# Weights packed in order of use, x and vectors turned by the host, and longer runs of high and low products

## The chip, the cores and the metric

The kernel runs on one core of a Trainium2 chip. The metric is the device time of one execution in microseconds. Five engines work side by side: PE (TensorE) multiplies matrices, PEld is its loading of the stationary operand, DVE (VectorE) and ACT (ScalarE) do elementwise work, POOL (GpSimd) and SP mostly start transfers (DMA). Each engine takes its instructions in order, and waits for others through semaphores.

## The reference, cut to what matters

```python
# T = 256 positions, D = 2048, D_FF = 5504, everything float32, one layer
h = rms_norm(x, norm_mix);  proj = h @ w_in                      # 2048 x 9216
uv, qkv, gates = split(proj)
u, v = split(gelu(uv));  y_a = u * (w_s @ layer_norm(v) + b_s)   # 8 groups, chunks of 128
y_b = neighbourhood_attn(q, k, v, rpb)                           # 16 heads on a 4 x 64 grid
merged = sigmoid(g_a) * (y_a @ w_branch[:1024]) + sigmoid(g_b) * (y_b @ w_branch[1024:])
x = x + merged @ w_out
up = conv3(rms_norm(x, norm_ffn) @ w_up) + conv_b                # 2048 x 11008
x = x + (silu(gate) * val) @ w_down                              # 5504 x 2048
out = rms_norm(x, norm_final)
```

Some 61 million weights are used once each.

## The kernel before

**Products in three parts.** TensorE multiplies in a rounded format (float32r). To keep float32's precision, weights and activations are each split into a high part, which is the value rounded, and a low part, which is the rest: `w = whi + wlo`, `x = xh + xl`. A product is then `xh whi + xl whi + xh wlo`. For weights ACT writes `whi` (L127) and DVE writes `wlo` (L128); for x the same is done at L318 and L325, with the norm's weight `gmix` multiplied in.

**Pieces.** All weights are cut into pieces of two k, that is of 2 x 128 rows by up to 512 columns, numbered in the order in which they are used. `begin(i)` opens piece i: it issues loads up to five pieces ahead of the splits (`load_to`, SP's queue, `wraw` with 5 buffers), splits up to three pieces ahead (`split_to`, `whi` and `wlo` with 4 buffers each), and runs what was noted for this piece with `at(i, f)`: transposes, evictions, softmax and so on. For the first five pieces the noted work comes ahead of the splits. In `load_to`, `preload[i]` is further loads that go into SP's queue ahead of piece i's weights.

**Two kinds of groups.** A group is one block of output columns over all k. In a *natural* group ("nat", `products`, L198 to L200) the activations are stationary and the weights stream 512 columns: per k and half of the positions three products, each of 512 columns. In a *weight-stationary* group ("ws", `spread_products`, L177 and L181) the weights are stationary: for each of up to four blocks of 128 columns a *high* product streams `xh` and `xl` together (512 columns, L177) and a *low* product streams `xh` alone (256 columns, L181). Per k all blocks' high products come first, then all blocks' low ones; for the last k of a group it is low, then high. Each block has its own PSUM bank. Weight-stationary are two u groups, four qk groups and 22 groups of the up-projection, with 16 k each; the last of these has two blocks instead of four.

**The start.** x is loaded in eight chunks of 256 columns with positions on partitions (`load_x`, L243, tile `xs`). Each chunk is turned by four transposes on TensorE (`x_chunk`, L338) into a PSUM bank, and split from there. Ahead of it TensorE runs transposes of the identity (`keep_awake`, L283), nine and then eight. The norm's weights, the convolution's and its bias are loaded as rows and turned likewise (`vec_T`, L257), and so is W_s (`turn_ws`, L870). The sum of squares of x for the norm is taken by ACT from `xs` at pieces 5 to 8 (`x_stats`).

Of the kernel before, what the change touches and what calls it, by code (L numbers as in the profile page):

```python
# [15 lines left out]
T = 256  # L16
# [22 lines left out]

LOAD_AHEAD = 5  # L40
# [3 lines left out]

@with_exitstack
def trunk_kernel(ctx, tc, x, norm_mix, w_in, ln_g, ln_b, w_s, b_s, rpb, w_branch, w_out,
                 norm_ffn, w_up, conv_k, conv_b, w_down, norm_final, out):
# [27 lines left out]
    pieces = []  # L75

    def plan(src, row0, nk, blocks):
        first = len(pieces)
        for k in range(0, nk, 2):
            pieces.append((src, row0 + k * 128, min(2, nk - k), blocks))  # L80
        return first
# [6 lines left out]
    def load_to(n):  # L88
        while n_loaded[0] < min(n, len(pieces)):
            i = n_loaded[0]  # L90
            n_loaded[0] += 1
            if i in preload:
                for f in preload[i]:
                    f()
            src, r0, kn, (c0, cn, nb, cs) = pieces[i]
            w = wpool.tile([128, 2, 512], F32, name="wraw", bufs=LOAD_AHEAD)
            ld = src.shape[-1]
            if i == 0:
                for k in range(kn):
                    if k:  # L100
                        load_x(256, 256)
                    nc.sync.dma_start(w[:, k, :cn], src[r0 + k * 128:r0 + (k + 1) * 128, c0:c0 + cn])
            elif nb == 1:
                nc.sync.dma_start(
                    w[:, :kn, :cn],
                    bass.AP(tensor=src.tensor, offset=src.offset + r0 * ld + c0,
                            ap=[[ld, 128], [128 * ld, kn], [1, cn]]))
            else:
                for b in range(nb):
                    nc.sync.dma_start(  # L110
                        w[:, :kn, b * cn:(b + 1) * cn],
                        bass.AP(tensor=src.tensor, offset=src.offset + r0 * ld + c0 + b * cs,
                                ap=[[ld, 128], [128 * ld, kn], [1, cn]]))
            raw[i] = w

    def split_to(n):
        while n_split[0] < min(n, len(pieces)):
            i = n_split[0]
            n_split[0] += 1
            src, r0, kn, (c0, cn, nb, cs) = pieces[i]  # L120
# [3 lines left out]
            m = cn * nb  # L124

            def part(k):
                nc.scalar.activation(h[:, k, :m], w[:, k, :m], AF.Copy)  # L127
                nc.vector.tensor_sub(l[:, k, :m], w[:, k, :m], h[:, k, :m].bitcast(F32))  # L128
# [15 lines left out]
    midway = {}  # L144
# [5 lines left out]
    def begin(i):  # L150
        cur[0] = i
        load_to(i + LOAD_AHEAD)
        if i == 0:
            gm_turn()
            split_to(1)
# [7 lines left out]
    def natural(src, row0, nk, c0, cn, acts, done):  # L163
        n0 = plan(src, row0, nk, (c0, cn, 1, 0))
        return ("nat", n0, nk, cn, acts, done)

    def stationary(src, row0, nk, c0, cn, nb, cs, acts, done):
        n0 = plan(src, row0, nk, (c0, cn, nb, cs))
        return ("ws", n0, nk, cn * nb, acts, done)

    def spread_products(g, ps, i, h, l):
# [30 lines left out]
    def run_group(g, by_block=0):  # L202
# [4 lines left out]
        for i in range(n0, n1 - by_block):  # L207
# [7 lines left out]
            for b in range(nblk):  # L215
                if b == 1 and i in midway:
                    midway.pop(i)()
# [22 lines left out]
    xs = xin.tile([128, NT, D], F32)  # L240

    def load_x(c0, n):
        nc.sync.dma_start(xs[:, :, c0:c0 + n],  # L243
                          bass.AP(tensor=x.tensor, offset=x.offset + c0, ap=[[D, 128], [128 * D, NT], [1, n]]))

    def rows(src, off, n):
        return bass.AP(tensor=src.tensor, offset=src.offset + off, ap=[[128, n], [1, 128]])

    def vec_T(name, src, off, n, dst, queue=None):
        t = xin.tile([n, 128], F32, name=name)  # L250

        def load():
            (queue or nc.sync).dma_start(t, rows(src, off, n))

        def go():
            p = bank()
            nc.tensor.transpose(p[:, :n], t, ident[:n, :n])  # L257
            nc.vector.tensor_copy(dst, p[:, :n])
        return load, go

    gmix = const.tile([128, KD], F32)
    gffn = const.tile([128, KD], F32)
    ck = const.tile([128, 4, 2 * NF], F32)
    gm_load, gm_turn = vec_T("gm_rows", norm_mix, 0, KD, gmix, nc.scalar)
    gm_load()
    ws_raw = xin.tile([128, GMG, 128], F32)

    def load_ws():
        nc.sync.dma_start(ws_raw, bass.AP(tensor=w_s.tensor, offset=w_s.offset,
                                          ap=[[128, 128], [128 * 128, GMG], [1, 128]]))  # L270
# [15 lines left out]
    late = [vec_T("gf_rows", norm_ffn, 0, KD, gffn)]  # L286
    for j in range(3):
        late.append(vec_T(f"ck_rows{j}", conv_k, j * 2 * DFF, 2 * NF, ck[:, j, :]))
    late.append(vec_T("cb_rows", conv_b, 0, 2 * NF, ck[:, 3, :]))
# [26 lines left out]
    def split_pair(p, dsts, gs):  # L316
# [3 lines left out]
        for kk in range(2):  # L320
# [12 lines left out]
    def x_chunk(c):  # L333
        p = bank()
        for kk in range(2):
            k = c * 2 + kk
            for t in range(NT):
                nc.tensor.transpose(p[:, kk * T + t * 128:kk * T + (t + 1) * 128],  # L338
                                    xs[:, t, k * 128:(k + 1) * 128], ident)
        split_pair(p, xT[2 * c:2 * c + 2], gmix[:, 2 * c:2 * c + 2])  # L340
# [9 lines left out]
    def ev_vg(j):  # L350
        def done(ps, i):
            if j == 0:
                at(i + 2, lambda: gelu_v(ps, i))
# [444 lines left out]
    w_in2 = w_in[0]  # L798
    w_br, w_o, w_u, w_d = w_branch[0], w_out[0], w_up[0], w_down[0]
    xt = lambda k: xT[k]  # L800
    g_vg = [natural(w_in2, 0, KD, V0 + j * 512, 512, xt, ev_vg(j)) for j in range(2)]
    g_u = [stationary(w_in2, 0, KD, U0 + j * 512, 512, 1, 0, xt, ev_u(j)) for j in range(2)]
    def g_va(j):
        return natural(w_in2, 0, KD, VA0 + j * 512, 512, xt, ev_va(j))

    def g_qk(j):
        return stationary(w_in2, 0, KD, Q0 + j * 256, 256, 2, K0 - Q0, xt, ev_qk(j))

    def g_gate(br, j):
        return natural(w_in2, 0, KD, (GA0, GB0)[br] + j * 512, 512, xt, ev_gate(br, j))  # L810

    def g_branch(br, j):
        return natural(w_br, br * 1024, 8, j * 512, 512, lambda k: yT[br * 8 + k], ev_branch(br, j))
# [6 lines left out]
    g_o = [natural(w_o, 0, KD, j * 512, 512, lambda k: mg["mT"][k], ev_out(j)) for j in range(4)]  # L820
    g_up = []
    for f in range(0, NF, 2):
        nb = min(2, NF - f)
        g_up.append(stationary(w_u, 0, KD, f * 128, nb * 128, 2, DFF, lambda k: rs["h", k], ev_up(f, nb)))
    g_dn = [natural(w_d, 0, NF, j * 512, 512, lambda k: ff["a"][k], ev_down(j) if j < 3 else finish) for j in range(4)]
# [24 lines left out]
    for c in range(4):  # L850
        at(5 + c, lambda c=c: x_stats(c))
    at(9, x_norm)
    at(12, lambda: st1.__setitem__("rb", bcast_cols("rb1", st1["r"])))
# [7 lines left out]
    preload[9] = [load_ws]  # L861
    for n, (dst, src) in enumerate(((gm_pool["g"], ln_g), (gm_pool["b"], ln_b),
                                    (gm_pool["bs"].rearrange("p a b -> p (a b)"), b_s))):
        preload[10 + n] = [lambda dst=dst, src=src: nc.sync.dma_start(
            dst, bass.AP(tensor=src.tensor, offset=src.offset, ap=[[0, 128], [1, GMW]]))]

    def turn_ws(h):
        p = bank()
        for g in range(4):
            nc.tensor.transpose(p[:, g * 128:(g + 1) * 128], ws_raw[:, h * 4 + g, :], ident)  # L870
        nc.vector.tensor_copy(gm_pool["wsT"][:, h * 4:h * 4 + 4, :].rearrange("p a b -> p (a b)"), p)

    at(14, lambda: turn_ws(0))
    at(15, lambda: turn_ws(1))
    preload[13] = [ld for ld, _ in late]
    for n, (_, f) in enumerate(late):
        at(17 + n // 2, f)
# [71 lines left out]
    for g in g_dn[:3]:  # L949
# [5 lines left out]
_INS = ['x', 'norm_mix', 'w_in', 'gm_ln_g', 'gm_ln_b', 'gm_w_s', 'gm_b_s', 'na_rpb', 'w_branch', 'w_out',  # L955
        'norm_ffn', 'w_up', 'conv_k', 'conv_b', 'w_down', 'norm_final']
# [24 lines left out]
```

## Time and profile before

| | |
|---|---|
| median of 3 runs | 1339.79 us (1339.69 to 1340.09) |
| span of the profiled execution, first to last instruction | 1338.0 us |
| its own time beside the span | not listed apart; the median lies 1.8 us above the span |
| PE busy | 1327.1 us, 99% |
| DVE, ACT, POOL busy | 871.8, 719.0, 104.8 us |
| moved by DMA | 259.36 MB, mean 194 GB/s |
| mean granted TensorE clock | 0.998 |
| first product of a piece starts | 6.49 us |
| first weight-stationary product starts | 56.96 us |

In rows of the timeline the first number is the start in us from the span's start, the second the time from the start of the first instruction of the row to the end of the last; `x4` means four instructions in the row. Matmuls overlap, since the next one starts while the last one drains. Names are tiles: `bank<-h,whi` writes a PSUM bank from the split activations and the weights' high part. In square brackets stand the idle time ahead and what ended it.

### The profile page before, as it was taken

The page shows a single profiled execution, that of the slowest core. Times are in us where ns is not written, and L with a number is a line of the kernel's source. Part 1 is how long each engine was busy: PE and PEld are TensorE (multiplying, and loading weights), DVE is VectorE, ACT ScalarE, POOL GpSimd, SP SyncE. Part 2 cuts the span into 40 slices and gives each one's busy share as a digit, 9 for nine tenths or more (in the row PEclk, how much of TensorE's full clock was granted, in tenths as well). Part 3 has the DMA queues.
Part 4 walks back from the last instruction along what each step waited for, and adds up shares of the span by engine and source line. Part 5 has one row for each costly group of instructions (what it writes and reads, how often), then busy time and mean ns, then how long its engine had stood idle before and what let it go on. Part 6 is the DMA issues. An engine that isn't in the chain of part 4 may idle for free.

```text
span 1338.0 us, 18985 instructions
## 1 busy us (share of the span) xinstructions
PE 1327.1 (99%) x6863; PEld 1127.8 (84%) x6863; DVE 871.8 (65%) x1256; ACT 719.0 (54%) x1059; POOL 104.8 (8%) x192
## 2 busy tenths in 40 slices
PE   9999999999999999999999999999999999999997
PEld 7888888888888888888888888888888888888885
DVE  6476567767564645555778777777777775545454
ACT  6665557577444444555655555555555554434342
POOL 0241055530000000000000000000000000000000
PEclk9999999999999999999999999999999999999999
DMA  9766775655666666665565656565656557656662
GB/s 329 223 188 179 215 224 173 205 173 161 196 182 194 190 192 222 204 197 183 185 192 182 196 177 200 177 196 182 192 186 190 172 181 225 209 186 208 188 198 101
DMA packets 194030, 259.36 MB, mean 194 GB/s; under 512 B 12952, under 2 KB 124432, under 8 KB 193936
## 3 DMA queue, kind: packets, MB, share of 16 engines
q1 hardware_dynamic: 189648, 250.31, 59.8%
q0 software_dynamic: 3968, 7.30, 2.3%
q8 instruction: 54, 0.88, 0.3%
q10 hardware_dynamic: 320, 0.53, 0.1%
q14 instruction: 40, 0.33, 0.1%
HBM read 253.90 MB, written 2.10 MB: 191 GB/s over the span
## 4 chain that ended last, share of the span: by engine, by line
PE 99%; DMA 0%; DVE 0%; ACT 0%; SPq 0%; issue 0%; DVEq 0%
PE bank L177 31%; PE bank L198 17%; PE bank L200 17%; PE bank L199 17%; PE bank L181 16%; PE bank L563 1%; DMA wraw<-in_w_in_dram 0%; PE bank L613 0%; PE bank L439 0%; PE bank L659 0%; PE bank L603 0%; PE bank L701 0%; PE bank L338 0%; DVE x L791 0%; PE bank L310 0%; PE bank L870 0%
## 5 line engine op out<-in xcount | busy, mean ns | idle before, releaser
L128 DVE TENSOR_TENSOR wlo<-wraw,whi 128x1024 fp32r<-128x1024 f32 (+1 forms) x473 | 570.6, 1211 | 395.2 <-ACT whi L127 381.4
L127 ACT ACTIVATE whi<-wraw 128x1024 fp32r<-128x1024 f32 (+1 forms) x473 | 491.8, 1044 | 414.9 <-PE bank L199 280.4
L177 PE MATMUL bank<-h,whi 128*128 128x512 f32 x1760 | 479.2, 395 | 0.0
L177 PEld LDWEIGHTS bank<-h,whi 128*128 128x128 f32 x1760 | 301.9, 189 | 41.5
L181 PEld LDWEIGHTS bank<-h,wlo 128*128 128x128 f32 x1760 | 267.2, 189 | 35.6
L181 PE MATMUL bank<-h,wlo 128*128 128x256 f32 x1760 | 276.6, 281 | 0.0
L198 PE MATMUL bank<-whi,h 128*128 128x512 f32 x384 | 152.4, 397 | 0.1
L199 PE MATMUL bank<-whi,h 128*128 128x512 f32 x384 | 149.9, 390 | 0.4 <-DVE h L325 0.3
L200 PE MATMUL bank<-wlo,h 128*128 128x512 f32 x384 | 149.9, 390 | 0.0
L199 PE MATMUL bank<-whi,a 128*128 128x512 f32 x344 | 133.8, 389 | 0.0
L200 PE MATMUL bank<-wlo,a 128*128 128x512 f32 x344 | 133.8, 389 | 0.0
L198 PE MATMUL bank<-whi,a 128*128 128x512 f32 x344 | 133.8, 389 | 0.0
L199 PEld LDWEIGHTS bank<-whi,h 128*128 128x128 f32 x384 | 72.3, 188 | 15.5 <-DVE h L325 1.2
L200 PEld LDWEIGHTS bank<-wlo,h 128*128 128x128 f32 x384 | 72.2, 188 | 15.6 <-DVE wlo L128 0.4
L198 PEld LDWEIGHTS bank<-whi,h 128*128 128x128 f32 x384 | 72.2, 188 | 15.0 <-ACT whi L127 0.5
L727 ACT ACTIVATE tc<-ta,ck 128x256 f32<-128x256 f32 x86 | 47.1, 595 | 69.8 <-DVE ta L725 69.8
L199 PEld LDWEIGHTS bank<-whi,a 128*128 128x128 f32 x344 | 64.6, 188 | 13.5
L200 PEld LDWEIGHTS bank<-wlo,a 128*128 128x128 f32 x344 | 64.6, 188 | 13.4
L198 PEld LDWEIGHTS bank<-whi,a 128*128 128x128 f32 x344 | 64.6, 188 | 13.3
L943 POOL DMA_DIRECT2D gfin<-in_norm_final_dram x4 | 2.2, 548 | 646.5 <-DVE tc L738 539.2
L730 DVE SCALAR_TENSOR_TENSOR tc<-ta,ck,tc 128x255 f32<-128x255 f32 x86 | 41.4, 481 | 14.4 <-ACT tc L727 14.4
L198 PE MATMUL bank<-whi,m 128*128 128x512 f32 x128 | 50.1, 392 | 0.0
(157 smaller groups left out, 1092.7 us busy)
## 6 DMA issues: line engine op xcount, KB each, us to landing
wraw<-in_w_up_dram SPq DMA_DIRECT2D x336, 256.0 KB, 3.2
wraw<-in_w_in_dram SPq DMA_DIRECT2D x111, 512.0 KB, 3.7
wraw<-in_w_down_dram SPq DMA_DIRECT2D x84, 512.0 KB, 4.6
wraw<-in_w_in_dram SPq DMA_DIRECT2D x66, 256.0 KB, 3.5
wraw<-in_w_branch_dram SPq DMA_DIRECT2D x32, 512.0 KB, 4.5
wraw<-in_w_out_dram SPq DMA_DIRECT2D x32, 512.0 KB, 3.9
xs<-in_x_dram SPq DMA_DIRECT2D x8, 256.0 KB, 7.2
vw<-va POOLq DMA_DIRECT2D x32, 64.0 KB, 5.2
```

The source lines that it names most:

```text
L127: nc.scalar.activation(h[:, k, :m], w[:, k, :m], AF.Copy)
L128: nc.vector.tensor_sub(l[:, k, :m], w[:, k, :m], h[:, k, :m].bitcast(F32))
L177: nc.tensor.matmul(p, h[:, k - k0, b * 128:(b + 1) * 128], acts(k), start=k == 0, stop=k == nk - 1)
L181: nc.tensor.matmul(p[:, :T], l[:, k - k0, b * 128:(b + 1) * 128], acts(k)[:, 0, :], start=False, stop=False)
L198: nc.tensor.matmul(p, xh, h[:, kk, :m], start=st, stop=False)
L199: nc.tensor.matmul(p, xl, h[:, kk, :m], start=False, stop=False)
L200: nc.tensor.matmul(p, xh, l[:, kk, :m], start=False, stop=sp)
L563: nc.tensor.matmul(o, Q[s][:, c], k.rearrange("p (r c) -> p r c", r=ROWS)[:, :, k0:k0 + UNION], start=n == 0, stop=n == 1)
L727: nc.scalar.activation(v, u, AF.Identity, scale=ck[:, 1, ch:ch + 1], bias=ck[:, 3, ch:ch + 1])
L730: nc.vector.scalar_tensor_tensor(v[:, 1:], u[:, :T - 1], ck[:, 0, ch:ch + 1], v[:, 1:], op0=OP.mult, op1=OP.add)
L943: nc.gpsimd.dma_start(fin["g", j], bass.AP(tensor=norm_final.tensor, offset=norm_final.offset + j * 512, ap=[[0, 128], [1, 512]]))
```

## The change

The host (numpy) now lays the inputs out before the launch:

- All weights lie in one flat array in the order of the pieces, and within a piece each partition's two k lie together, so one partition's part is one run of 4 KB (in before rows of 2 KB, or of 1 KB in groups with two column blocks). A piece is one transfer, where groups with two column blocks took two.
- x comes turned (`x_turned`, k on partitions, loaded by k). `x_chunk` splits straight from SBUF; the transposes of x are gone. The statistics still need x by rows, which is loaded a second time, in two transfers of 1 MB ahead of the weights of pieces 10 and 11. They are taken at pieces 9 to 12 instead of 5 to 8, the norm at 13 instead of 9, and the first gelu moves from two pieces behind its group to six.
- The vectors come turned in one array: 16 columns at the start on ACT's queue, the rest ahead of the weights of piece 16. W_s comes turned, ahead of piece 12. `vec_T` and `turn_ws` are gone with their transposes and copies.
- In a weight-stationary piece the high products of both k come together, then the low ones; in every second piece low ones first, then high ones.

```diff
-        for k in range(k0, min(k0 + 2, nk)):
-            for f in (high, low) if k < nk - 1 else (low, high):
+        for f in (high, low) if (i - n0) % 2 == 0 else (low, high):
+            for k in range(k0, min(k0 + 2, nk)):
                 f(k)
...
+            cn = size // kn
+            parts = range(kn) if i == 0 else [slice(0, kn)]
+            for k in parts:
+                k0, k1 = (k, k + 1) if i == 0 else (0, kn)
+                if i == 0 and k:
+                    load_x(1)
+                src = bass.AP(tensor=weights.tensor, offset=weights.offset + off + k0 * cn,
+                              ap=[[size, 128], [cn, k1 - k0], [1, cn]])
+                nc.sync.dma_start(w[:, k0:k1, :cn], src)
...
+    def load_x(k0, n=1):
+        nc.sync.dma_start(xk[:, k0:k0 + n, :], x_turned[:, k0:k0 + n, :])
...
-    def x_chunk(c):
-        p = bank()
-        for kk in range(2):
-            k = c * 2 + kk
-            for t in range(NT):
-                nc.tensor.transpose(p[:, kk * T + t * 128:kk * T + (t + 1) * 128],
-                                    xs[:, t, k * 128:(k + 1) * 128], ident)
-        split_pair(p, xT[2 * c:2 * c + 2], gmix[:, 2 * c:2 * c + 2])
+    def x_chunk(c, part=(0, 1)):
+        split_pair(xk[:, 2 * c:2 * c + 2, :].rearrange("p k t -> p (k t)"), xT[2 * c:2 * c + 2],
+                   gmix[:, 2 * c:2 * c + 2], part)
...
-    preload[0] = [lambda: load_x(0, 256)]
-    for c in range(2, 8):
-        preload[c] = [lambda c=c: load_x(256 * c, 256)]
-    at(0, lambda: x_chunk(0))
+    preload[0] = [lambda: load_x(0)]
+    for c in range(1, 8):
+        preload[c] = [lambda c=c: load_x(2 * c, 2)]
+    at(0, lambda: x_chunk(0, (0,)))
     at(0, lambda: first["rest"]())
+    at(0, lambda: x_chunk(0, (1,)))
     at(0, lambda: keep_awake(WAKE[1]))
-    midway[0] = lambda: x_chunk(1)
+    at(0, lambda: x_chunk(1))
     for c in range(2, 8):
         at(c - 1, lambda c=c: x_chunk(c))
+    for t in range(NT):
+        preload[10 + t] = [lambda t=t: load_rows(t)]
```

The first place is PE in the up-projection, where one group ends and the next begins; `h` is the split activations of one k, `x4` the four column blocks. Before:

```order
L177 MATMUL bank<-h_5802,whi 128x512 x4
L181 MATMUL bank<-h_5802,wlo 128x256 x4
L177 MATMUL bank<-h_5812,whi 128x512 x4
L181 MATMUL bank<-h_5812,wlo 128x256 x4
L181 MATMUL bank<-h_5813,wlo 128x256 x4
L177 MATMUL bank<-h_5813,whi 128x512 x4
L177 MATMUL bank<-h_5218,whi 128x512 x4
L181 MATMUL bank<-h_5218,wlo 128x256 x4
```

Now, in the first pieces of the first such group:

```order
L235 MATMUL bank<-h_5107,whi 128x512 x4
L235 MATMUL bank<-h_5108,whi 128x512 x4
L239 MATMUL bank<-h_5107,wlo 128x256 x4
L239 MATMUL bank<-h_5108,wlo 128x256 x4
L239 MATMUL bank<-h_5118,wlo 128x256 x4
L239 MATMUL bank<-h_5119,wlo 128x256 x4
L235 MATMUL bank<-h_5118,whi 128x512 x4
L235 MATMUL bank<-h_5119,whi 128x512 x4
```

Runs of four high and four low products, with runs of eight where groups meet, have become runs of sixteen each.

The second place is the start of the program on PE. Before:

```order
L283 MATMUL bank<-ident 128x128 x9
L257 MATMUL bank<-ident,gm_rows 128x16
L338 MATMUL bank<-ident,xs 128x128 x4
L283 MATMUL bank<-ident 128x128 x8
L198 MATMUL bank<-whi,h_109 128x512
L199 MATMUL bank<-whi,h_109 128x512
L200 MATMUL bank<-wlo,h_109 128x512
```

Now:

```order
L321 MATMUL bank<-ident 128x128 x17
L256 MATMUL bank<-whi,h_101 128x512
L257 MATMUL bank<-whi,h_101 128x512
L258 MATMUL bank<-wlo,h_101 128x512
```

The transposes that waited for loads are gone from among the 17 of the identity.

The third place is SP's queue, from the last chunk of x on. Before:

```order
L243 DMA xs<-in_x_dram 128x2x256
L104 DMA wraw<-in_w_in_dram 128x2x512 x2
L269 DMA ws_raw<-in_gm_w_s_dram 128x8x128
L104 DMA wraw<-in_w_in_dram 128x2x512
L864 DMA lng<-in_gm_ln_g_dram 128x1024
```

Now:

```order
L300 DMA xk<-in_x_turned_dram 128x512
L177 DMA wraw<-in_weights_dram 128x1024 x3
L303 DMA xs<-in_x_dram 128x2048
L177 DMA wraw<-in_weights_dram 128x1024
L303 DMA xs<-in_x_dram 128x2048
L177 DMA wraw<-in_weights_dram 128x1024
L888 DMA wsT<-in_w_s_turned_dram 128x1024
```

Two transfers of x by rows stand ahead of W_s, which moves three pieces back.

More of the change, by code (lines that the diff above doesn't have):

```diff
@@ L38 @@
 LN_EPS = 1e-5
+BLOCK = 1024
 LOAD_AHEAD = 5
@@ L42, with weight_groups, add, gate @@
 WAKE = (9, 8)
+def weight_groups():
+    g = []
+    def add(key, w, row0, nk, *blocks):
+        g.append((key, w, row0, nk, blocks))
+    def gate(br, j):
+        add(("gate", br, j), "w_in", 0, KD, ((GA0, GB0)[br] + j * 512, 512))
+    def branch(br, j):
+        add(("branch", br, j), "w_branch", br * 1024, 8, (j * 512, 512))
+    def qk(j):
+        add(("qk", j), "w_in", 0, KD, (Q0 + j * 256, 256), (K0 + j * 256, 256))
+    for j in range(2):
+        add(("vg", j), "w_in", 0, KD, (V0 + j * 512, 512))
+    for j in range(2):
+        add(("u", j), "w_in", 0, KD, (U0 + j * 512, 512))
+    for j in range(2):
+        add(("va", j), "w_in", 0, KD, (VA0 + j * 512, 512))
+        qk(j)
+    gate(0, 0)
+    qk(2)
+    gate(1, 0)
+    qk(3)
+    gate(0, 1)
+    gate(1, 1)
+    for j in range(2):
+        branch(0, j)
+        branch(1, j)
+    for j in (2, 3):
+        gate(0, j)
+        gate(1, j)
+        branch(0, j)
+        branch(1, j)
+    for j in range(4):
+        add(("out", j), "w_out", 0, KD, (j * 512, 512))
+    for f in range(0, NF, 2):
+        nb = min(2, NF - f) * 128
+        add(("up", f), "w_up", 0, KD, (f * 128, nb), (DFF + f * 128, nb))
+    for j in range(4):
+        add(("down", j), "w_down", 0, NF, (j * 512, 512))
+    return g
@@ new lines, in weight_pieces, with packed_weights @@
+def weight_pieces():
+    out, starts, at = [], {}, 0
+    for key, w, row0, nk, blocks in weight_groups():
+        starts[key] = len(out)
+        cols = sum(n for _, n in blocks)
+        per = max(1, BLOCK // cols) if BLOCK % cols == 0 and cols > 256 else 2
+        for k in range(0, nk, per):
+            kn = min(per, nk - k)
+            out.append((w, row0 + k * 128, kn, blocks, at, kn * cols))
+            at += 128 * kn * cols
+    return out, starts, at
+def packed_weights(arrays):
+    import numpy as np
+    pieces, _, total = weight_pieces()
+    flat = np.empty(total, np.float32)
+    for w, r0, kn, blocks, at, n in pieces:
+        rows = arrays[w][0, r0:r0 + kn * 128].reshape(kn, 128, -1)
+        d = flat[at:at + 128 * n].reshape(128, kn, -1)
+        c = 0
+        for c0, cn in blocks:
+            d[:, :, c:c + cn] = rows[:, :, c0:c0 + cn].transpose(1, 0, 2)
+            c += cn
+    return flat
@@ L45, in trunk_kernel @@
 @with_exitstack
-def trunk_kernel(ctx, tc, x, norm_mix, w_in, ln_g, ln_b, w_s, b_s, rpb, w_branch, w_out,
-                 norm_ffn, w_up, conv_k, conv_b, w_down, norm_final, out):
+def trunk_kernel(ctx, tc, x, x_turned, weights, vectors, ln_g, ln_b, w_s_turned, b_s, rpb, norm_final, out):
     nc = tc.nc
@@ L72, in bank @@
         return psum.tile([128, 512], F32, name="bank")
[L75 to L81, printed above, removed]
+    pieces, starts, _ = weight_pieces()
+    counts = {key: nk for key, _, _, nk, _ in weight_groups()}
     raw, split_t = {}, {}
@@ L94, in load_to @@
                     f()
-            src, r0, kn, (c0, cn, nb, cs) = pieces[i]
+            _, _, kn, _, off, size = pieces[i]
             w = wpool.tile([128, 2, 512], F32, name="wraw", bufs=LOAD_AHEAD)
[L97 to L113, printed above, removed]
+            cn = size // kn
[7 more added lines that the diff above has]
+                nc.sync.dma_start(w[:, k0:k1, :cn], src)
             raw[i] = w
@@ L119, in split_to @@
             n_split[0] += 1
-            src, r0, kn, (c0, cn, nb, cs) = pieces[i]
+            _, _, kn, _, _, size = pieces[i]
             w = raw.pop(i)
@@ L161, in begin, with group @@
             run_tasks(i)
[L163 to L169, printed above, removed]
+    def group(kind, key, acts, done):
+        n = pieces[starts[key]]
+        return (kind, starts[key], counts[key], n[5] // n[2], acts, done)
     def spread_products(g, ps, i, h, l):
@@ L240, in trunk_kernel, with load_rows @@
     xs = xin.tile([128, NT, D], F32)
[L242 to L255, printed above, removed]
-            p = bank()
[L257 to L270, printed above, removed]
+    xk = xin.tile([128, KD, T], F32)
+    def load_x(k0, n=1):
+        nc.sync.dma_start(xk[:, k0:k0 + n, :], x_turned[:, k0:k0 + n, :])
+    def load_rows(t):
+        nc.sync.dma_start(xs[:, t, :], x[0, t * 128:(t + 1) * 128, :])
+    vec = const.tile([128, 2 * KD + 8 * NF], F32)
+    gmix, gffn = vec[:, :KD], vec[:, KD:2 * KD]
+    ck = vec[:, 2 * KD:].rearrange("p (j f) -> p j f", j=4)
+    nc.scalar.dma_start(gmix, vectors[:, :KD])
     one = const.tile([128, 1], F32)
@@ L285, in trunk_kernel @@
     keep_awake(WAKE[0])
[L286 to L289, printed above, removed]
     def rstd(name, ssum, n, eps):
@@ L860, in trunk_kernel @@
     gm_pool["bs"] = G.tile([128, GMG, 128], F32, name="bsb")
-    preload[9] = [load_ws]
+    preload[12] = [lambda: nc.sync.dma_start(gm_pool["wsT"], w_s_turned)]
+    preload[16] = [lambda: nc.sync.dma_start(vec[:, KD:], vectors[:, KD:])]
     for n, (dst, src) in enumerate(((gm_pool["g"], ln_g), (gm_pool["b"], ln_b),
                                     (gm_pool["bs"].rearrange("p a b -> p (a b)"), b_s))):
-        preload[10 + n] = [lambda dst=dst, src=src: nc.sync.dma_start(
+        preload[13 + n] = [lambda dst=dst, src=src: nc.sync.dma_start(
             dst, bass.AP(tensor=src.tensor, offset=src.offset, ap=[[0, 128], [1, GMW]]))]
[L867 to L877, printed above, removed]
     for g in g_vg:
```

69 lines of the change are left out of this document (36 added, 33 removed).

## The prediction

> **What bounds the kernel now.** I read the page's busy rows and the chain of work that ended last first, to learn whether any engine but TensorE sets the end.
>
> ```profile
> span 1338.0 us, 18985 instructions
> ...
> PE 1327.1 (99%) x6863; PEld 1127.8 (84%) x6863; DVE 871.8 (65%) x1256; ACT 719.0 (54%) x1059; POOL 104.8 (8%) x192
> ...
> PE 99%; DMA 0%; DVE 0%; ACT 0%; SPq 0%; issue 0%; DVEq 0%
> ```
>
> TensorE is on the chain for 99% of the span. So a transfer that gets faster, or DVE and ACT work that goes, is worth nothing by itself; only what TensorE issues, the time between two of its products, and its few waits at the start count. The span is 1338.0 us and the median of the runs 1339.79; I take the 1.8 us around the span as unchanged and subtract from the median.
>
> Busy time does not tell what a product costs, since matmuls overlap (each shown as 0.39 us long). The starts in the timeline of PE do. In a "natural" stretch:
>
> ```profile
> 600.00 0.39 PE L199 MATMUL bank<-whi,m 128*128 128x512 f32 x1
> ...
> 605.66 0.39 PE L200 MATMUL bank<-wlo,m 128*128 128x512 f32 x1
> ```
>
> 25 products lie between these rows: 5.66 / 25 = 0.2264 us per 512-column product (0.2267 over longer stretches, the value used below). This is the steady rate, and the change does not touch it. In the weight-stationary stretch of the up-projection:
>
> ```profile
> 880.04 1.12 PE L181 MATMUL bank<-h,wlo 128*128 128x256 f32 x8
> 880.99 2.00 PE L177 MATMUL bank<-h,whi 128*128 128x512 f32 x8
> 882.84 0.64 PE L181 MATMUL bank<-h,wlo 128*128 128x256 f32 x4
> 883.31 1.09 PE L177 MATMUL bank<-h,whi 128*128 128x512 f32 x4
> 884.24 0.63 PE L181 MATMUL bank<-h,wlo 128*128 128x256 f32 x4
> 884.71 1.09 PE L177 MATMUL bank<-h,whi 128*128 128x512 f32 x4
> ```
>
> A low product alone is 0.28 us long, so eight of them in 1.12 start (1.12 - 0.28) / 7 = 0.120 us apart. Now compare: one high-low turn of 4 + 4 takes 884.71 - 883.31 = 1.40 us (1.4025 from the groups below), against 4 x 0.2267 + 4 x 0.120 = 1.387 at steady rates. Each turn thus costs 0.016 us beyond its products. The rows of eight stand where two groups meet, since the last k of a group already goes low, high. That turn takes 882.84 - 880.04 = 2.80 for a base of 2.773: 0.026 us for twice the products. The trace of before already holds the change's pattern in small.
>
> **The change, part one: longer runs.** 27 full groups (two u, four qk, 21 up) and one half-wide last one are weight-stationary. A group takes, from the chain of waits:
>
> ```profile
> 791.40 1.84 PE bank L177 x8
> ...
> 813.84 1.84 PE bank L177 x8
> ```
>
> 22.44 us for 16 k, while the steady rates give 16 x 1.3867 = 22.187: 0.253 us per group goes into turns. The new order in one piece is high, high, low, low, and in the next low, low, high, high; the runs become 16 + 16, four turns per group. What a turn of 16 + 16 costs no row shows. From below: nothing, which saves 0.253 x 27.5 = 7.0 us. From above: it grows with the run's length as it did from 4 to 8, 0.026 x 0.026 / 0.016 = 0.042, so 22.187 + 4 x 0.042 = 22.355, which saves 0.085 x 27.5 = 2.3 us. I take 0.026: the high run of eight lasts 882.84 - 880.99 = 1.85 against 8 x 0.2267 = 1.81, and a run of four already 0.93 against 0.907, so 0.023 of some 0.036 is spent in the first half; the excess fades inside the run, and its second half is nearly steady. Then a group takes 22.187 + 4 x 0.026 = 22.29 and the gain is 0.15 x 27.5 = **4.1 us**.
>
> No buffer turns short by it: the split is written three pieces ahead, 8.4 us at 2.8 us per piece, while it takes these two operations, one after the other:
>
> ```profile
> L128 DVE TENSOR_TENSOR wlo<-wraw,whi 128x1024 fp32r<-128x1024 f32 (+1 forms) x473 | 570.6, 1211 | 395.2 <-ACT whi L127 381.4
> L127 ACT ACTIVATE whi<-wraw 128x1024 fp32r<-128x1024 f32 (+1 forms) x473 | 491.8, 1044 | 414.9 <-PE bank L199 280.4
> ```
>
> 2.3 us. Were that lead gone, each piece would pay up to those 2.3 us.
>
> **Part two: transposes leave TensorE.** A chunk of x costs four transposes and a late next product:
>
> ```profile
> 14.45 0.60 PE L338 MATMUL bank<-ident,xs 128*128 128x128 f32 x4
> 14.80 0.48 PE L198 MATMUL bank<-whi,h 128*128 128x512 f32 x1
> 15.12 0.39 PE L199 MATMUL bank<-whi,h 128*128 128x512 f32 x1
> ...
> 50.55 0.60 PE L870 MATMUL bank<-ident,ws_raw 128*128 128x128 f32 x4
> 50.90 0.48 PE L198 MATMUL bank<-whi,h 128*128 128x512 f32 x1
> 51.22 0.39 PE L199 MATMUL bank<-whi,h 128*128 128x512 f32 x1
> ```
>
> From 14.45 to 15.12 is 0.67; one product of it remains: 0.44 us per chunk. Five chunks come behind piece 1: 2.2 us. W_s costs the same (51.22 - 50.55 - 0.227 = 0.44), twice: 0.9. The vectors' five transposes stretch three pieces:
>
> ```profile
> 59.27 0.63 PE L181 MATMUL bank<-h,wlo 128*128 128x256 f32 x4
> ...
> 61.08 0.63 PE L181 MATMUL bank<-h,wlo 128*128 128x256 f32 x4
> ...
> 62.46 0.64 PE L181 MATMUL bank<-h,wlo 128*128 128x256 f32 x4
> ...
> 64.04 0.64 PE L181 MATMUL bank<-h,wlo 128*128 128x256 f32 x4
> ```
>
> 1.81 - 1.40 and 1.58 - 1.40 for two each, some 0.15 for the fifth: 0.7. Their copies on DVE and the loads on SP's queue cost nothing, as nothing on the chain waited for them.
>
> **Part three: the start.** These rows pace the first two pieces:
>
> ```profile
> 4.82 1.91 PE L283 MATMUL bank<-ident 128*128 128x128 f32 x8
> ...
> 5.45 0.63 ACT L127 ACTIVATE whi<-wraw 128x512 fp32r<-128x512 f32 x1 [2.71 <-DMA wraw<-in_w_in_dram]
> ...
> 6.49 0.80 PE L198 MATMUL bank<-whi,h 128*128 128x512 f32 x1
> ...
> 9.00 1.06 ACT L127 ACTIVATE whi<-wraw 128x1024 fp32r<-128x1024 f32 x1 [0.72 <-DMA wraw<-in_w_in_dram]
> ...
> 10.10 1.23 DVE L128 TENSOR_TENSOR wlo<-wraw,whi 128x1024 fp32r<-128x1024 f32 x1 [1.09 <-ACT whi L127]
> ...
> 11.59 0.48 PE L198 MATMUL bank<-whi,h 128*128 128x512 f32 x1
> ...
> 12.14 0.40 PE L200 MATMUL bank<-wlo,h 128*128 128x512 f32 x1
> ...
> 27.63 0.48 PE L198 MATMUL bank<-whi,h 128*128 128x512 f32 x1
> ...
> 28.40 0.50 PE L199 MATMUL bank<-whi,h 128*128 128x512 f32 x1 [0.29 <-DVE h L325]
> ```
>
> The first k of x now comes alone, 131 KB less ahead of the first weights; at the 285 GB/s of the table below that is 0.46 us, so the first product moves from 6.49 to about 6.0. The second weights have 262 KB less ahead and come about 0.9 us sooner, so piece 0 ends near 9.8. But the whole of piece 1 has the same bytes ahead as before: landed at 9.00, its high half on ACT to 10.06, its low half to 11.33. Its third product needs that low half: 11.33 instead of 12.14, a lead of **0.8 us**, bounded by 0 and 1.8 (if piece 1 could follow 9.8 at once). Behind it a piece takes 12 x 0.2267 = 2.72 instead of 3.16. The split of x still runs on ACT and DVE, from SBUF instead of PSUM, in the same order; at piece 6 it waits behind four weight splits, which cost 0.5 us at 27.63. TensorE now comes faster to that point, but the x statistics are out of ACT's way there. I leave that wait as it is (bounds: gone, 0.5 gained; doubled, 0.5 lost).
>
> x as rows for the statistics comes a second time, 2.1 MB, behind pieces 9 and 10:
>
> ```profile
> 4.30:7.70 3.40, 3.31 (x14) 2.64 (x13) 1.55 (x3) 1.40 (x4) 0.00 (x0) 1.00 0.88 285
> ...
> 6.00:33.00 27.00, 26.53 (x125) 20.76 (x124) 19.65 (x28) 20.09 (x39) 0.00 (x0) 1.00 1.04 366
> 33.00:57.00 24.00, 24.00 (x113) 19.88 (x113) 12.44 (x18) 14.16 (x23) 2.95 (x7) 1.00 0.73 237
> ```
>
> (last columns: clock, DMA share, GB/s.) The transfers are at their limit, 366 GB/s, until 33 us. Up to the weights of piece 16 the queue now holds 17 x 0.524 + 4.2 (x twice) + 2.5 (W_s, LN and vectors) = 15.6 MB. With 1 MB there at 6 us, 366 GB/s brings the rest by 46 us; TensorE wants piece 16 at about 52 and its split 2.3 us earlier: nearly 4 us to spare. Cost nothing.
>
> One loss remains: the 17 wake-up transposes now run in one piece, 0.213 us apart (1.91 - 0.42 over 7), 1.38 to 5.0, and TensorE then stands idle for 1 us. In before the x transposes stood among them, and the row at 14.45 shows four in 0.60, twice the rate. If the slow rate returns, the first products start twice as slowly; but piece 1 waits for 11.33 anyway. I take 0.3 us lost, between 0 and 2.5 (eleven products of 0.227).
>
> Sum: 4.1 + 2.2 + 0.9 + 0.7 + 0.8 - 0.3 = **8.4 us**; 1339.8 - 8.4 = **1331.4**.
>
> **The rivals.**
> *Runs gain nothing* (the order changes, the time per k does not): 1335.5. For it: the excess grew from 0.016 to 0.026 with the run. Against: it less than doubled. 0.10.
> *The clock stays low at the start.* For it: 1 us idle and a start paced by loads; against: piece 1 waits for its weights longer than the slow products last. 2.5 instead of 0.3 lost: 1333.6. 0.12. The Trainium skill (TensorE: Matmul & The Clock Gate, Part 1) has the clock rise after about 3.4 us of sustained work and fall after an idle window as long; by it 3.6 us of wake-ups just fill one window, and whether the first products run fast depends on where the window lies: 1331.1 if it is filled, this rival if not. The trace agrees that the rate doubles after some 5 us of work (the rows at 4.82 and 14.45); no row here shows a fall inside the kernel.
> *Transfers starve the start* (the slower side): the 2.1 MB of rows go ahead of piece 10's weights in one queue. Piece 16 is late below 14.6 / 43.7 = 333 GB/s; below 14.6 / 52.1 = 280 the whole gain is gone; at 260 the loss is 12.5 us and the time 1343.9. For it: 237 GB/s in the last row. Against: loads waited for buffers there, and 366 held for 27 us. 0.04.
>
> **How the numbers follow.** The forecast has 0.72, the rivals 0.10, 0.12, 0.04, and 0.02 is left for what I do not see. Both faster rivals stay inside the range: its lower end is 1339.8 - 7.0 - 4.6 = 1328.2, rounded to 1328.0 (the other good ends of the start, 1.8 us in all, would have to come on top of the best case of the runs); its upper end 1339.8 - 2.3 - (4.6 - 2.5) = 1335.4, rounded up to 1335.6 to hold the first rival. A measurement of this kernel tells 0.2% (2.7 us) from no change: the first three cases are faster, starvation is half slower, half same, and overlapping bad ends of the others (no run gain and a cold start: 1337.7) add to same. Faster 0.92, same 0.05, slower 0.03.
>
> **What would show it.** Right: in the up stretch rows of x16, low about 2.08 long (15 x 0.120 + 0.28), high about 3.82 (15 x 0.2267 + 0.03 + 0.39), and groups 22.29 apart; piece 16 (first weight-stationary product) at about 53 instead of 56.96; no idle on PE behind 30 us. Wrong: groups 22.36 to 22.44 apart; first products 0.45 apart beyond 10 us; PE waiting for ACT or DMA between 25 and 55 us.

## The result, and the profile after

The changed kernel takes 1331.72 us (median of four runs, 1330.86 to 1332.15) where the kernel before took 1339.74 in the same comparison: a ratio of 0.9938, 95% interval 0.9924 to 0.9952. That is 8.0 us, or 0.6%; 8.4 had been forecast. The profiled execution's span went from 1338.0 to 1329.9 us, 8.1 us.

The page of the changed kernel, its busy rows and its chain of work:

```profile
span 1329.9 us, 18442 instructions
...
PE 1317.1 (99%) x6817; PEld 1124.5 (85%) x6817; DVE 868.5 (65%) x1248; ACT 721.8 (54%) x1059; POOL 100.2 (8%) x192
...
PE 98%; DMA 1%; DVE 0%; SPq 0%; ACT 0%; issue 0%; DVEq 0%
...
DMA packets 77082, 261.40 MB, mean 197 GB/s; under 512 B 9792, under 2 KB 13760, under 8 KB 76736
```

TensorE still is the bound, with 46 instructions fewer (6863 to 6817: 32 transposes of x, 8 of W_s, 6 of vectors). The packets fell from 194030 to 77082.

The timeline of PE in the up-projection, where before had rows of x4:

```profile
854.78 2.08 PE L239 MATMUL bank<-h,wlo 128*128 128x256 f32 x16
856.69 3.82 PE L235 MATMUL bank<-h,whi 128*128 128x512 f32 x16
860.35 2.08 PE L239 MATMUL bank<-h,wlo 128*128 128x256 f32 x16
862.26 3.82 PE L235 MATMUL bank<-h,whi 128*128 128x512 f32 x16
```

The lengths 2.08 and 3.82 are the forecast ones. A turn of 16 + 16 takes 862.26 - 856.69 = 5.57 us (5.566 over longer stretches), a base of 16 x 0.2267 + 16 x 0.120 = 5.547: a turn costs 0.019 us, not the 0.026 that I took. The whole up-projection, from its first product to the first product of the down-projection, went from 483.71 us (611.33 to 1095.04) to 480.10 (606.70 to 1086.80). The two ends of it, before and now:

```profile
611.33 1.07 PE L177 MATMUL bank<-h,whi 128*128 128x512 f32 x4
...
1095.04 0.39 PE L198 MATMUL bank<-whi,a 128*128 128x512 f32 x1
```

```profile
606.70 1.98 PE L235 MATMUL bank<-h,whi 128*128 128x512 f32 x8
...
1086.80 0.39 PE L256 MATMUL bank<-whi,a 128*128 128x512 f32 x1
```

The start, from the timelines of ACT, DVE and PE:

```profile
1.38 3.89 PE L321 MATMUL bank<-ident 128*128 128x128 f32 x17 [1.38 <-POOL ident masks.py:199]
...
4.93 0.79 PE L256 MATMUL bank<-whi,h 128*128 128x512 f32 x1
...
9.06 1.06 ACT L191 ACTIVATE whi<-wraw 128x1024 fp32r<-128x1024 f32 x1 [1.33 <-DMA wraw<-in_weights_dram]
...
10.15 1.22 DVE L192 TENSOR_TENSOR wlo<-wraw,whi 128x1024 fp32r<-128x1024 f32 x1 [1.71 <-ACT whi L191]
...
11.43 0.50 PE L258 MATMUL bank<-wlo,h 128*128 128x512 f32 x1 [0.53 <-DVE wlo L192]
...
14.53 0.50 PE L258 MATMUL bank<-wlo,h 128*128 128x512 f32 x1
...
26.06 0.50 PE L257 MATMUL bank<-whi,h 128*128 128x512 f32 x1 [0.58 <-DVE h L359]
...
53.67 1.98 PE L235 MATMUL bank<-h,whi 128*128 128x512 f32 x8
```

The chain of piece 1 stands as forecast: landed at 9.06 (9.00 forecast), third product at 11.43 (11.33 forecast, 12.14 before). Two waits follow: at piece 2's third product, 0.25 us (it starts at 14.53, the one before it at 14.05), and at piece 6, where 0.29 us of idle time became 0.58. The first weight-stationary product came from 56.96 to 53.67. The transfers by stretches of time (last columns: clock, DMA share, GB/s):

```profile
6.00:33.00 27.00, 24.63 (x102) 18.58 (x101) 18.79 (x26) 18.04 (x27) 0.00 (x0) 1.00 1.01 397
33.00:57.00 24.00, 24.00 (x115) 20.18 (x114) 12.23 (x17) 19.27 (x37) 10.95 (x23) 1.00 0.94 324
```

397 GB/s instead of 366, and the second copy of x shows as 324 instead of 237 GB/s between 33 and 57 us, with PE busy through all 24 us.

### The profile page after: what moved, and what is told of

Same layout as the page of the kernel before. It is cut to its first block, busy times and chain, and to the rows that moved or that the text cites. A ratio compares the mean times of both kernels' runs of the same rounds, so it can differ in the third digit from the quotient of the medians.

```text
span 1329.9 us, 18442 instructions
## 1 busy us (share of the span) xinstructions
PE 1317.1 (99%) x6817; PEld 1124.5 (85%) x6817; DVE 868.5 (65%) x1248; ACT 721.8 (54%) x1059; POOL 100.2 (8%) x192
## 4 chain that ended last, share of the span: by engine, by line
PE 98%; DMA 1%; DVE 0%; SPq 0%; ACT 0%; issue 0%; DVEq 0%
PE bank L235 30%; PE bank L256 17%; PE bank L258 17%; PE bank L257 17%; PE bank L239 16%; DMA wraw<-in_weights_dram 1%; PE bank L592 1%; PE bank L642 0%; PE bank L468 0%; PE bank L730 0%; PE bank L688 0%; PE bank L632 0%; SPq L300 0%; DVE x L820 0%; SPq L177 0%; DVE wlo L192 0%
## 5 line engine op out<-in xcount | busy, mean ns | idle before, releaser
L235 PE MATMUL bank<-h,whi 128*128 128x512 f32 x1760 | 423.1, 391 | 0.0
L235 PEld LDWEIGHTS bank<-h,whi 128*128 128x128 f32 x1760 | 322.9, 188 | 61.7
L239 PEld LDWEIGHTS bank<-h,wlo 128*128 128x128 f32 x1760 | 226.4, 191 | 9.0
L239 PE MATMUL bank<-h,wlo 128*128 128x256 f32 x1760 | 230.8, 283 | 0.0
L756 ACT ACTIVATE tc<-ta,vec 128x256 f32<-128x256 f32 x86 | 47.1, 595 | 70.1 <-DVE ta L754 70.1
L746 ACT ACTIVATE tb<-bank 128x256 f32<-128x256 f32 x86 | 28.3, 384 | 43.0 <-PE bank L235 42.7
L759 DVE SCALAR_TENSOR_TENSOR tc<-ta,vec,tc 128x255 f32<-128x255 f32 x86 | 41.4, 481 | 14.4 <-ACT tc L756 14.4
```

The source lines that it names most:

```text
L235: nc.tensor.matmul(p, h[:, k - k0, b * 128:(b + 1) * 128], acts(k), start=k == 0, stop=k == nk - 1)
L239: nc.tensor.matmul(p[:, :T], l[:, k - k0, b * 128:(b + 1) * 128], acts(k)[:, 0, :], start=False, stop=False)
L746: nc.scalar.activation(t, p[:, T:], AF.Copy)
L756: nc.scalar.activation(v, u, AF.Identity, scale=ck[:, 1, ch:ch + 1], bias=ck[:, 3, ch:ch + 1])
L759: nc.vector.scalar_tensor_tensor(v[:, 1:], u[:, :T - 1], ck[:, 0, ch:ch + 1], v[:, 1:], op0=OP.mult, op1=OP.add)
```

## The experiments

**The order alone.** The kernel before, with only the order of products changed:

```diff
-        for k in range(k0, min(k0 + 2, nk)):
-            for f in (high, low) if k < nk - 1 else (low, high):
+        for f in (high, low) if (i - n0) % 2 == 0 else (low, high):
+            for k in range(k0, min(k0 + 2, nk)):
                 f(k)
```

> The kernel before with nothing but the new order of high and low products in the weight-stationary pieces (runs of 16 + 16). Theory: a turn between a high and a low run costs about 0.02 us however long the runs are, so the time goes with the number of turns; fewer of them give the 4.2 us that the weight-stationary stretches of the changed kernel gained: 1335.5 us, groups of the up-projection 22.27 us apart instead of 22.44. Rival: the longer runs only pay with the packed weights (one transfer per piece): 1338 or more.

Measured: 1335.72 us beside 1339.82 for the kernel before, ratio 0.9968 (0.9957 to 0.9979): 4.1 us. The timeline of PE:

```profile
855.11 3.82 PE L177 MATMUL bank<-h,whi 128*128 128x512 f32 x16
858.76 2.08 PE L181 MATMUL bank<-h,wlo 128*128 128x256 f32 x16
860.68 3.82 PE L177 MATMUL bank<-h,whi 128*128 128x512 f32 x16
```

5.57 us per turn as in the changed kernel, with weights unpacked, and an up-projection of 480.10 us to the hundredth. So half of the gain is the order's, and needs nothing of the rest; the other half (1335.72 to 1331.72) is the start and the transposes.

**Runs of eight.** The changed kernel, with high products first in every piece but a group's last:

```diff
-        for f in (high, low) if (i - n0) % 2 == 0 else (low, high):
+        for f in (high, low) if k0 + 2 < nk else (low, high):
```

> The changed kernel, but every piece has its high products first (the last piece of a group its low ones), so runs are 8 + 8 and a group has 8 turns instead of 4. Theory (cost per turn): a group takes 22.187 + 8 x 0.026 = 22.40 instead of 22.27 us; in all about 3 us more than the changed kernel: 1334.8. Rival (what counts is that the two k of a piece are taken together, not where the next piece begins): no slower than the changed kernel, 1331.7.

Measured: 1333.04 us (0.9948, 0.9935 to 0.9962). Neither number came: slower than the changed kernel by 1.3, not by 3. Its chain of waits (start, length, count):

```profile
852.48 3.65 PE bank L235 x16
856.13 0.95 PE bank L239 x8
857.09 1.84 PE bank L235 x8
858.93 0.95 PE bank L239 x8
859.88 1.84 PE bank L235 x8
```

A turn of 8 + 8 takes 859.88 - 857.09 = 2.79 us, 0.02 beyond its base of 2.773, not 0.026. And a group has seven turns, not eight, since where groups meet the runs are of sixteen: 22.187 + 7 x 0.02 = 22.33 us instead of 22.27 with four turns, 1.3 us in 21 groups; the up-projection took 481.40 us, 1.3 more than with 16 + 16. Theory and size then agree: the cost goes by turns. The rows also show where it lies: sixteen highs take 3.65, eight 1.84, so the second eight take 1.81 = 8 x 0.2267, steady; all of the excess (1.84 - 1.814) stands in the first eight behind a turn. The low runs give a little back, 0.95 instead of 0.96 for eight.

Why had the rows of before said 0.026? The chain of waits of before, where two groups meet:

```profile
880.20 0.96 PE bank L181 x8
881.16 1.84 PE bank L177 x8
```

The eight low products stood there behind a run of only four high ones. The eight high products behind them take the same 1.84 as here, but the eight lows take 0.96 where they take 0.95 behind a longer high run, at every such place of the up-projection. So what they gave back was missing: it was a mixed turn.

**Runs of 32.** Two pieces of the up-projection multiplied together, all high products of four k, then all low ones, in turns; the splits then go two pieces at a time:

```diff
+            for i in range(n0, n1, 2):
+                begin(i)
+                begin(i + 1, True)
+                hl = [split_t.pop(i), split_t.pop(i + 1)]
...
+        for f in (high, low) if (i - n0) % 4 == 0 else (low, high):
+            for k in range(k0, k0 + 4):
+                f(k)
```

> The changed kernel with two pieces of the up-projection multiplied together: runs of 32 + 32, two turns per group. Theory (a turn costs 0.019 us, as the rows of 8 + 8 and 16 + 16 both show): 2 x 0.019 x 21.5 = 0.8 us less, the up-projection from 480.1 to 479.3 us, 1330.9. Rival (the cost grows with the run): nothing, 480.1.

Measured: 1332.33 us (0.9944, 0.9931 to 0.9956), no faster than the changed kernel. The timeline of PE, in mid-stretch and at the end of the up-projection:

```profile
859.35 7.44 PE L254 MATMUL bank<-h,whi 128*128 128x512 f32 x32
866.63 4.00 PE L260 MATMUL bank<-h,wlo 128*128 128x256 f32 x32
870.46 7.44 PE L254 MATMUL bank<-h,whi 128*128 128x512 f32 x32
...
1083.06 1.34 PE L260 MATMUL bank<-h,wlo 128*128 128x256 f32 x8 [0.42 <-DVE wlo L192]
...
1087.72 0.50 PE L279 MATMUL bank<-wlo,a 128*128 128x512 f32 x1 [0.91 <-DVE wlo L192]
```

The turn costs what it cost: 870.46 - 859.35 = 11.11 against a base of 11.094. What the fewer turns gave was lost at the end. The splits run up to three pieces ahead, but two pieces held together take a part of that lead; the last group is half as wide, its pieces last half as long, and TensorE waited for low halves, in that group and in the first piece of the down-projection. That the pairs took the lead is argued here; the last version below, which leaves the pairs out at the end, bears it out. The distances between products there are 0.6 and 1.1 us longer than usual, and the part of the span behind the up-projection is 1.3 us longer than in the changed kernel (244.4 instead of 243.1).

**Unpacked weights.** The changed kernel, with the weights read from their own matrices as before:

```diff
-                src = bass.AP(tensor=weights.tensor, offset=weights.offset + off + k0 * cn,
-                              ap=[[size, 128], [cn, k1 - k0], [1, cn]])
-                nc.sync.dma_start(w[:, k0:k1, :cn], src)
+                c = 0
+                for c0, n in blocks:
+                    nc.sync.dma_start(
+                        w[:, k0:k1, c:c + n],
+                        bass.AP(tensor=src.tensor, offset=src.offset + (r0 + k0 * 128) * ld + c0,
+                                ap=[[ld, 128], [128 * ld, k1 - k0], [1, n]]))
+                    c += n
```

> The changed kernel with the weights read from their own matrices as before (rows of 2 KB or 1 KB, two transfers for pieces with two column blocks). Theory: the transfers are off the chain but for pieces 1 to 3, which start 0.5 us or less behind their splits; at 366 instead of 397 GB/s their weights land 0.3 to 0.6 us later: 1332.2, at most 1332.6. Rival: the packing carries a part of the gain in the rest of the kernel too: 1333.5 or more.

Measured: 1331.97 us (0.9940, 0.9928 to 0.9953), not told from the changed kernel. The two timelines agree in the up-projection (480.10 us). At the start the transfers were slower, and the first weight-stationary product came at 54.64 instead of 53.67. (In the profiled executions of the four versions that share the changed kernel's start it came between 53.02 and 53.99.) The transfers by stretches:

```profile
6.00:33.00 27.00, 24.33 (x98) 18.11 (x99) 18.98 (x26) 17.34 (x26) 0.00 (x0) 1.00 1.02 382
...
700.00:1000.00 300.00, 300.00 (x1727) 265.17 (x1726) 234.21 (x381) 176.65 (x270) 0.00 (x0) 1.00 0.62 189
```

Packing all weights, the largest part of the diff, is worth at most the first microsecond; with TensorE as the bound nothing was to be had from it.

**No wake-up.** The changed kernel without its 17 transposes of the identity:

```diff
-WAKE = (9, 8)
+WAKE = (0, 0)
```

> The changed kernel without the 17 transposes of the identity that TensorE runs before its first product. Theory: the first products run at half rate until about 9 us, but piece 1 waits for its weights' low half until 11.4 anyway: 0 to 0.6 us lost, 1332.0. Rival (a cold start costs in full): the rate stays low until 12 us or more and the products of pieces 0 and 1 lose 2 us: 1334.

Measured: 1331.61 us (0.9937, 0.9924 to 0.9949). The timeline of PE:

```profile
5.03 0.80 PE L256 MATMUL bank<-whi,h 128*128 128x512 f32 x1 [5.03 <-ACT h L352]
...
10.18 0.63 PE L258 MATMUL bank<-wlo,h 128*128 128x512 f32 x1
10.60 0.63 PE L256 MATMUL bank<-whi,h 128*128 128x512 f32 x1
...
12.55 0.40 PE L258 MATMUL bank<-wlo,h 128*128 128x512 f32 x1
12.79 0.39 PE L256 MATMUL bank<-whi,h 128*128 128x512 f32 x1
...
15.33 0.39 PE L258 MATMUL bank<-wlo,h 128*128 128x512 f32 x1
...
25.98 0.39 PE L257 MATMUL bank<-whi,h 128*128 128x512 f32 x1
```

The products ran at half rate, 0.43 us apart, until 12.3 us, longer than I had expected, and it cost nothing by the first weight-stationary product, which came at 53.46. But the wait for piece 1's low half did not hide all of it: piece 1's third product came at 12.55 instead of 11.43, 1.1 us late. The wait at piece 2 (0.25 us in the changed kernel) took a part, and its third product came at 15.33 instead of 14.53, 0.8 late. The rest went at piece 6, where the changed kernel waits for DVE's split of x: that product came at 25.98, without a wait, instead of 26.06. So the cold start is hidden behind three waits, and the last one is for DVE and not for weights. With the start mended as below these waits are gone; what the cold start costs there was not measured. The Trainium skill (TensorE: Matmul & The Clock Gate, Part 1) gives about 3.4 us of sustained work for the clock to rise; here it took 7.3 us from the first product, with gaps of up to 0.6 us among the first ones, and 4.7 us from the end of the last such gap (7.58).

**The rows of x early.** The changed kernel with the 2.1 MB of x by rows ahead of the weights of pieces 3 and 4, and ahead of the chunks of turned x that go before these weights:

```diff
-        preload[10 + t] = [lambda t=t: load_rows(t)]
+        preload[3 + t] = [lambda t=t: load_rows(t)] + preload[3 + t]
```

> The changed kernel with the 2.1 MB of x by rows ahead of the weights of pieces 3 and 4 instead of 10 and 11. Theory (starvation is a matter of place: pieces 2 to 4 have 0.5 to 1.2 us between split and use, pieces 10 and later several): each megabyte costs 2.65 us at 397 GB/s, of which piece 3 has 0.5 to spare and piece 4 1.2; about 3.6 us more than the changed kernel: 1335.3. Rival (loads run far enough ahead everywhere): 1331.7.

Measured: 1336.35 us (0.9974, 0.9964 to 0.9983), 4.6 more than the changed kernel. Two timelines, of ACT and of PE:

```profile
14.83 0.91 ACT L352 ACTIVATE h<-xk,vec 128x256 fp32r<-128x256 f32 x2 [2.12 <-DMA xk<-in_x_turned_dram]
...
19.27 0.91 ACT L352 ACTIVATE h<-xk,vec 128x256 fp32r<-128x256 f32 x2 [2.11 <-DMA xk<-in_x_turned_dram]
```

```profile
17.21 0.50 PE L256 MATMUL bank<-whi,h 128*128 128x512 f32 x1 [0.58 <-ACT whi L191]
...
21.75 0.50 PE L256 MATMUL bank<-whi,h 128*128 128x512 f32 x1 [0.72 <-ACT whi L191]
```

The starvation that was the slow rival is real seven pieces earlier in the same queue: ACT waits 2.1 us for each megabyte, and TensorE behind it. I had forecast 3.6. Set against the changed kernel's, the starts of the products fall back by 3.5 us through pieces 3 and 4, and then by 1.5 more at piece 6, where TensorE waits longer for the split of x; this execution had been 0.5 ahead at piece 2. So the transfers cost what was said, and what I had not counted is the chunk of x at piece 6. Ahead of pieces 10 and 11 the same bytes cost nothing that the trace shows.

**The start mended.** The splits of pieces 1 to 3 in two halves, and the split of x ahead of the weights' at pieces 5 and 6:

```diff
-            if i:
+            if 1 <= i <= 3:
+                part(slice(0, 1))
+                part(slice(1, 2))
+            elif i:
                 part(slice(0, kn))
...
-        if i < 5:
+        if i < 7:
             run_tasks(i)
```

> The changed kernel with the splits of pieces 1 to 3 done in two halves, and the splits of x ahead of the weights' splits at pieces 5 and 6 too. Theory: the third product of piece 1 (11.43 us) waits for a low half made of the whole piece; half a piece is there about 1 us sooner, piece 2 follows, and the wait of 0.5 us at piece 6 goes: 1.5 us less than the changed kernel, 1330.2. Rival (the transfers pace these pieces, so a sooner piece 1 only waits at piece 2 or 4): 0.5 us or less, 1331.2.

Measured: 1330.83 us (0.9932, 0.9919 to 0.9944), 0.9 less than the changed kernel; in the profiled executions 2.0 less (span 1327.9). The timeline of PE through the third product of piece 1:

```profile
10.27 0.40 PE L259 MATMUL bank<-whi,h 128*128 128x512 f32 x1
10.50 0.39 PE L260 MATMUL bank<-whi,h 128*128 128x512 f32 x1
10.73 0.39 PE L261 MATMUL bank<-wlo,h 128*128 128x512 f32 x1
```

No wait is left at pieces 1, 2 and 6; the third product comes at 10.73 instead of 11.43, and the first weight-stationary one at 51.69 instead of 53.67: 0.8 us of that is gained by the fourth product of piece 1, 0.4 at piece 2 and 0.9 at piece 6. The start differs between executions: the first weight-stationary product came between 53.02 and 53.99 in the four versions with the changed kernel's start, and at 51.69, 52.12 and 52.22 in the three with the mended one. So the gain is shown, while its size, 0.9 to 2, stays open.

**All of it.** First the two edits to the start and the runs of 32 together:

> The two edits to the start and the runs of 32 together. Theory: the gains add, 2.3 us less than the changed kernel: 1329.4.

Measured: 1331.70 us (0.9939, 0.9925 to 0.9952): the loss at the end of the up-projection came back, and took the gain of the start. Then the same with runs of 32 in all groups but the last two:

```diff
-        if kind == "ws" and g in g_up:
+        if kind == "ws" and g in g_up[:-2]:
             for i in range(n0, n1, 2):
```

> The two edits to the start, and runs of 32 in the up-projection but for its last two groups, which go as in the changed kernel. Theory: the runs of 32 save 0.019 us per turn as their rows show, and lost it at the end of the up-projection, where the splits of the half-wide last group came late (0.6 us and, in the first down piece, 1.3 us); with the splits' lead back there, 19 x 2 x 0.019 = 0.7 us less than with the edits to the start alone: 1330.1. Rival (the pairs cost something in every group): 1330.8 or more.

Measured: 1330.10 us (0.9925, 0.9912 to 0.9939). Beside it on the same chip the changed kernel itself:

> The changed kernel itself, unaltered, beside the version above on one chip. Expected 1331.7.

1331.49 us (0.9935, 0.9922 to 0.9947). The up-projection of the mended version takes 479.3 us, 0.8 less than 480.1, its chain of waits:

```profile
703.03 7.28 PE bank L257 x32
710.31 3.83 PE bank L263 x32
714.14 7.28 PE bank L257 x32
```

and the rest of the span behind it is 243.2 us again; the first weight-stationary product comes at 52.12 beside 53.63. This is the fastest version, 1.4 us below the changed kernel beside it; the two intervals overlap, while the rows show where the time went.

## Why the prediction was right

**Runs: 4.1 us forecast, 4.1 measured** (the order alone). By luck two errors of size cancelled. A turn was taken at 0.026 us, from the rows where groups meet; it costs 0.019, whether the runs are 8, 16 or 32 long. That made the up-projection gain 3.6 us instead of 21.5 x 0.15 = 3.2. And the 0.15 per group was taken for all groups alike, where the six groups ahead of the up-projection gained 0.6 together and not 0.9: the qk groups between which attention runs went only from 24.63 to 24.55 us, 0.08, since their runs are cut by the transposes and products of attention, which stand between pieces (so the rows read; no run tests it apart). The first qk group, with nothing between, gained 0.17 (22.44 to 22.27). The half-wide last group, taken as half of one, gained nothing. Its rows before:

```profile
1084.34 0.40 PE L181 MATMUL bank<-h,wlo 128*128 128x256 f32 x2
...
1094.09 0.64 PE L181 MATMUL bank<-h,wlo 128*128 128x256 f32 x4
```

These are 14 turns of 2 + 2, each (1094.09 - 1084.34) / 14 = 0.696 us for a base of 0.693. A turn so short cost 0.003 us, and fewer turns of 0.019 us saved nothing: the group took 11.15 us before and 11.17 now. So the cost does grow with the run at first, 0.003, 0.016 and 0.019 us from 2 to 4 to 8, and then stays; the prediction's step that the excess fades inside the run holds.

**Transposes: 2.2 + 0.9 + 0.7 forecast.** They are gone, and the time to the first weight-stationary product fell by 3.3 us, where 2.2 + 0.9 + 0.8 (start) - 0.3 (clock) = 3.6 had been said. From piece 1's third product to the first weight-stationary one it took 44.82 us before (12.14 to 56.96) and 42.24 now (11.43 to 53.67), 2.6 less: the forecast 2.2 + 0.9, less some 0.45 by which the waits at pieces 2 and 6 grew. The two u groups, where the vectors' transposes had stood, fell from 47.23 to 46.33 us, 0.9: 0.7 and the turns.

**The start: 0.8 forecast, 0.7 measured at piece 1.** The step that failed is the first product: said to come at 6.0, it came at 4.93, since the first weights landed by 3.85 and not 5.0. It made no difference, as the prediction's own next step said: piece 1 waits for its low half. What was missed is the wait at piece 2 (0.25 us); of piece 6 it was said that its wait stays, within 0.5; it grew by 0.2. Pieces that last 2.72 us instead of 3.16 come closer to ACT and DVE, which need the same time for each as before.

**The clock: 0.3 forecast, nothing found** in the changed kernel, where only the first product is slow (0.79 us long at 4.93); without any wake-up the kernel is as fast. The rows named for a rise after some 5 us of work, at 4.82 and 14.45, only bound it: in the timeline of before the products turn fast between 7.38 (0.65 us long) and 7.87 (0.39 us), some 6 us after the first transpose at 1.38. The rival that priced a cold start at 2.5 us had the slow products right and the cover wrong. But the prediction's own reason, that piece 1 waits anyway, covers only a part: without wake-up 1.1 us were left behind it, and it was luck that the waits at pieces 2 and 6 took them up.

**Transfers: no cost forecast, none found** at pieces 10 and 11, and 4.6 us for the same bytes at pieces 3 and 4. The 366 GB/s that were read as the transfers' limit were not one: 397 came with the packed weights, so there was more to spare than counted. Packing the weights was costed at nothing, and is worth nothing that the times show.

## What to carry to other kernels

Where one engine is the bound, look at the distance between the starts of its instructions in each pattern that the trace already holds, even if it holds it only where two groups meet; then check that the rows compared are of the same kind on both sides. Packing all weights was worth nothing that the times show, turning x and the vectors was worth the transposes that it took off the bound engine, and two lines that change an order were worth half the gain: cost each part by what the bound engine issues. And a lead between engines that is counted in pieces shrinks when pieces are held together or become shorter; the place to look is where piece sizes change.

## What the runs showed of the hardware

- A turn between runs of 512-column and 256-column products costs TensorE 0.019 us, wherever the runs are at least eight long (0.016 for 4 + 4, 0.003 for 2 + 2); behind the turn the first eight high products take 1.84 instead of 1.81 us, and the next ones are steady. Why the first ones are slower no run here tells.
- Over 27 us of the start (6 to 33 us) the transfers moved 397 GB/s with the weights in rows of 4 KB and 382 with the same loads but the weights in rows of 2 KB. The kernel before, at 366, had weights in rows of 2 KB too and x in other rows.
- A TensorE at half rate for its first 7 us cost nothing in this start, since waits at pieces 1, 2 and 6 took up the time.
